# Retention values for all heads first, tokens on partitions, kept in DRAM; sums of output weights beside them

## The chip, the cores and the metric

The kernel runs on one core of a Trainium2 chip. The metric is device microseconds of one execution, the median of several. TensorE (PE in the profile) multiplies; VectorE (DVE) and ScalarE (ACT) add, split and move; GpSimd (POOL) does a few small powers; SyncE (SP) issues the DMAs, all on one queue and in program order. DRAM is reached only by DMA; PE writes PSUM banks of 128 x 512 float32, which DVE or ACT empty.

## The reference

A sequence of 1024 tokens with 1024 features goes through a retention layer and then an attention layer, in float32. The change is in the first:

```
h = rmsnorm(x, g_pre)
q, k, v, gate = split(h @ w_in)         # 1024, 1024, 2048, 2048 columns; 8 heads
q, k = rope(q), rope(k) * 128**-0.5     # a head: q, k of 128 columns, v of 256
for every chunk of 64 tokens, in order:
    inner = (q k^T * inner_dec) v
    cross = (q R) * xi;  R = R * g_c + (k * zeta)^T v
o = groupnorm(inner + cross) * gn_gain  # per head
y = (silu(gate) * o) @ w_out
h = x + rmsnorm(y, g_post)
```

The second layer (latent attention with shared keys and values) reads h and is left as it is.

## The kernel before

**Arithmetic.** A float32 product is made as three matmuls of a high and a low part of each operand (`mm3`, L180). So every operand is split first: ACT rounds it to the high part, DVE subtracts to get the low one (`split`, L187, rows of L189 and L190). On top lies one level of a Strassen-like scheme: a 2 x 2 block product needs seven products instead of eight, with sums of blocks on both sides. On the left these are sums of x's blocks (S1 to S4), on the right sums of weight blocks (T1 to T4), and the results are combined in the bank or by additions on DVE.

**Column pairs.** Layer A's input projection runs over 24 column pairs, three a head: q with k, the two halves of v, the two halves of the gate. Results have features on partitions and tokens along the row. `pair` (L343) runs a pair's seven products, its steps a to g; a `product` (L331) is 12 matmuls of 128 x 512. `Units` (L53) fetches a pair's weights (wraw, two loads of 512 KB), makes T1 to T4 (wsum) and splits each of the seven operands into a unit. Pair 0 is run plainly, with four units and eight products (`plain`, L405), and pairs 1 and 2 (EARLY) in an order that can start before the second half of the tokens is in.

**Heads.** A pair's results go to a sink. The steps of a head's retention are queued from there: `later(n, f)` runs f after n more products, and every product calls `tick`. Per half of the tokens: `ret_scores` transposes k and makes the scores; `ret_values` (L589) brings the values, made with features on partitions (`sink_v`, L524), to tokens on partitions by eight PE transposes (L599) and splits them; `ret_states` updates R; `ret_mix` multiplies, normalises, and its tail transposes y (L694), gates it and stores it to DRAM (yd). So a head's retention runs between the products of the next pairs, and a head is worked off in the time of 21 products.

**Output.** `prepare_out_a` (L720), called before the last pair, queues loads of yl (from yd) and wl (output weights) and makes the sums of the weights on DVE in that pair (L749 to L751; the last, L795, in the output itself). `out_a` runs seven products of four blocks, each of 24 matmuls.

**Order and buffers.** The order on an engine is fixed when the program is built: a scheduler arranges the instructions of the engines within the dependences that the code gives. Large tiles come from one heap of 51 blocks of 128 x 1024 float32, given out again in the order in which they were freed.

Of the kernel before, what the change touches and what calls it, by code (L numbers as in the profile page):

```python
# [18 lines left out]
P = 128  # L19
# [33 lines left out]
class Units:  # L53
# [6 lines left out]
    def __init__(self, T, order, source, ahead, early=0, plain=()):  # L60
# [3 lines left out]
        self.hold = sum(p < early for p, _ in order) - 2  # L64
        self.plain = plain
        self.pairs = list(dict.fromkeys(p for p, _ in order))
        self.raw, self.sums, self.made, self.left, self.ready = {}, {}, {}, {}, deque()

    def fetch(self):
# [12 lines left out]
        self.left[p] = {"r0": 2, "r1": 2} if p in self.plain else {"r0": 3, "r1": 5, "ta": 3, "tb": 3}  # L82
# [28 lines left out]
    def prep(self):  # L111
# [8 lines left out]
        name = {"B11": "r0", "B12": "r0", "B21": "r1", "B22": "r1", "T1": "ta", "T3": "ta", "T2": "tb", "T4": "tb"}[what]  # L120
# [10 lines left out]
    def next(self):  # L131
        if not self.ready:
            self.prep()
        u = self.ready.popleft()
        self.fill()

        if self.at < len(self.order):
            n = self.pairs.index(self.order[self.at][0]) + 2
            if self.at < self.hold:
                n = min(n, self.early)  # L140
            while self.n_fetched < min(n, len(self.pairs)):
                self.fetch()
        return u

# [4 lines left out]
class Trunk:  # L149
# [121 lines left out]
    def run(self):  # L271
# [4 lines left out]
        self.h1 = dp.tile([NT, P, DM], F32, name="h1")  # L276
        self.yd = [[dp.tile([P, DM], F32, name=f"yd{h}_{half}") for half in range(2)] for h in range(NH)]
# [53 lines left out]
    def product(self, ps, units, name, more=False, over=False, unit=None):  # L331
        u = units.next() if unit is None else unit
# [4 lines left out]
        if unit is None:  # L337
            self.heap.free(u)
# [38 lines left out]
    def layer_a(self):  # L377
# [4 lines left out]
        EARLY = 3  # L382
        order = [(0, w) for w in ("B11", "B12", "B21", "B22")]
        order += [(p, w) for p in range(1, EARLY) for w in ("B11", "B21")]
        order += [(p, "T2") for p in range(1, EARLY)]
        order += [(p, w) for p in range(1, EARLY) for w in ("T3", "T4")]
        order += [(p, w) for p in range(1, EARLY) for w in ("T1", "B22")]
        order += [(p, w) for p in range(EARLY, 3 * NH) for w in WINOGRAD]
        units = Units(self, order, lambda p: (I["w_in_a"][p], None), 3, EARLY, (0,))
        self.X, A = {}, {}  # L390
        rows = [[heap.get("xt") for _ in range(HT)] for _ in range(2)]
        for half in range(2):
            for t in range(HT):
                nc.sync.dma_start(rows[half][t], I["x"][half * HALF + t * P:half * HALF + (t + 1) * P, :])
            units.fetch()
        self.rows_norm(rows[0])
        self.rows_in(0, rows[0], A)
        sinks = [(h, kind) for h in range(NH) for kind in "qvg"]
        make = lambda p: getattr(self, "sink_" + sinks[p][1])(sinks[p][0])
        self.heads = [{"h": h} for h in range(NH)]  # L400

        first = make(0)
        us = [units.next() for _ in range(4)]

        def plain(i):  # L405
            banks = [self.bank("acc") for _ in range(2)]
            for m in range(2):
                for j in range(2):
                    self.product(banks[j], units, f"A{i + 1}{m + 1}", more=m > 0, unit=us[2 * m + j])
                    if m:  # L410
                        first(i, j, banks[j], None)

        plain(0)
        self.rows_norm(rows[1])
        pairs = [(make(p), {}) for p in range(1, EARLY)]
        for sink, st in pairs:
            self.pair(units, sink, "ae", st)
            if sink is pairs[0][0]:
                self.rows_in(1, rows[1], A)
                ret = self.small([P, 16], "ret")  # L420
                nc.sync.dma_start(ret, I["ret"])
                self.zeta, self.geps = ret[:, 0:8], ret[:, 8:16]
                self.cs = [heap.get("cos"), heap.get("sin")]
                for i in range(2):
                    nc.sync.dma_start(self.cs[i], I["ropea"][i])
        self.left_sum(A, "S2")
        plain(1)
        heap.free(*us, *[b for hl in self.X.pop("A21") for b in hl])
        for steps, w in (("b", "S3"), ("cf", "S4"), ("dg", None)):
            if w:  # L430
                self.left_sum(A, w)
            for sink, st in pairs:
                self.pair(units, sink, steps, st)
        for p in range(EARLY, 3 * NH):
            if p == 3 * NH - 1:
                self.prepare_out_a()
            self.pair(units, make(p), over=p == 3 * NH - 1)
# [12 lines left out]
    def rows_in(self, half, rows, A):  # L450
# [3 lines left out]
        for n in names:  # L454
            A["S1" if n == "A22" else n] = [heap.get("xa") for _ in range(2)]
            self.X[n] = [(heap.get("xhi", F32R), heap.get("xlo", F32R)) for _ in range(2)]
# [5 lines left out]
        for k in range(KD):  # L462
            if half:
# [7 lines left out]
            hi, lo = self.X[n][m]  # L471
            self.split_scaled(hi[:, c], lo[:, c], pt, g)
# [14 lines left out]
    def sink_q(self, h):  # L487
# [4 lines left out]
        def sink(i, j, bank, U):  # L492
# [4 lines left out]
            if cb[i][1] == 2:  # L497
                st["qk", i] = cb[i][0]
                if h:
                    self.rotate_a(cb[i][0], i)  # L500
                else:
                    self.later(7, lambda: self.rotate_a(cb[i][0], i))
                if i == 0:
                    dm = st["dmask"] = self.small([P, P], "dm", bufs=2)
                    self.nc.sync.dma_start(dm, self.I["dmask"][:, h * P:(h + 1) * P])
                    if h:
                        self.later(4, lambda: self.ret_scores(st, 0))
                        self.later(15 if h < NH - 1 else 11, lambda: self.ret_scores(st, 1))
# [14 lines left out]

    def sink_v(self, h):  # L524
        st = self.heads[h]
        vt = {}

        def sink(i, j, bank, U):
            if i not in vt:
                vt[i] = [self.heap.get("vt"), 0]  # L530
            self.take(vt[i][0][:, j * HALF:(j + 1) * HALF], bank, U)
            vt[i][1] += 1
            if vt[i][1] == 2:
                st["vt", i] = vt[i][0]
                if i == 0:
                    if h == 0:
                        self.later(1, lambda: self.ret_scores(st, 0))
                        self.later(8, lambda: self.ret_scores(st, 1))
                    wait = (2, 4, 6, 10, 12, 14) if h < NH - 1 else (1, 2, 5, 3, 6, 8)
                    for n, (what, half) in zip(wait, [(w, i) for i in range(2) for w in  # L540
                                                      (self.ret_values, self.ret_states, self.ret_mix)]):
                        self.later(n, lambda what=what, half=half: what(st, half))

        return sink
# [43 lines left out]

    def ret_values(self, st, half):  # L589

        nc, heap = self.nc, self.heap
        vt = st["vt", half]
        hi, lo = st["v", half] = heap.get("vhi", F32R), heap.get("vlo", F32R)
        for m in range(2):
            pt = self.bank("r", (P, 2, 256))
            for i in range(2):
                for e in range(2):
                    c = e * HALF + (2 * m + i) * P
                    nc.tensor.transpose(pt[:, i, e * P:(e + 1) * P], vt[:, c:c + P], self.ident)  # L599
            c = slice(m * HALF, (m + 1) * HALF)  # L600
            self.split(hi[:, c], lo[:, c], pt.rearrange("p a b -> p (a b)"))
# [118 lines left out]
    def prepare_out_a(self):  # L720
# [19 lines left out]
        K = [{"uses": 2} for _ in range(4)]  # L740

        def weights(b):
            k = K[b]
            k["b11"], k["b12"], k["b22"] = right(0, 0, b), right(0, 1, b), right(1, 1, b)

        def sums(b):
            k = K[b]
            k["t1"] = heap.get("t1")
            sub(k["t1"], k["b12"], k["b11"])  # L749
            sub(k["b12"], k["b22"], k["b12"])  # L750
            sub(k["b22"], k["b22"], k["t1"])  # L751
            k["t3"], k["t2"] = k.pop("b12"), k.pop("b22")
            used(b)

        def used(b):
            K[b]["uses"] -= 1
            if not K[b]["uses"]:
                heap.free(K[b].pop("b11"))

        for b in range(4):  # L760
            self.later(2 + 3 * b, lambda b=b: weights(b))
            self.later(3 + 3 * b, lambda b=b: sums(b))

        def load(prod, b):
            k = K[b]
            if prod == 1:
                k["a11"] = left(0, 0, b)
            elif prod == 6:
                k["a21"], k["a22"], k["a11"] = left(1, 0, b), left(1, 1, b), left(0, 0, b)
            elif prod == 4:  # L770
                k["a22"], k["b21"] = left(1, 1, b), right(1, 0, b)
# [5 lines left out]
        def make(prod, b):  # L777
            k = K[b]
            if prod == 1:
                u = two(k["a11"], k["b11"], k.pop("a11"))  # L780
                used(b)
                return u
# [660 lines left out]
```

## Time and profile before

| | us |
|---|---|
| median of 3 runs (1293.27 to 1294.65) | 1294.58 |
| the profiled execution | 1292.86 |
| its span in the trace | 1291.1 |
| PE busy | 1257.4 |
| DVE busy | 1001.7 |
| ACT busy | 642.8 |

The profile is of one execution; times inside it are counted from its span's start. Layer A's projection and retention run from the start to 598.67 us, where the first output product begins; the output and the second layer follow. A row of a group shows line, engine, operation, output and inputs by the names of the program, count, busy time, mean duration, and idle time before with what ended it. In a timeline row the bracket holds the idle time before it and its releaser. Matmuls overlap: one may show 0.39 us and yet follow the one before by 0.23.

### The profile page before, as it was taken

What the parts mean: (1) busy time and instruction counts of PE and PEld (TensorE: products, weight loads), DVE (VectorE), ACT (ScalarE), POOL (GpSimd) and SP (SyncE); (2) the same over time, 40 slices, a digit from 0 to 9 for tenths busy, and PEclk for the clock granted to TensorE, in tenths of its full rate; (3) what the DMA queues carried; (4) which work ended last, traced back from release to release, by engine and by line L of the source; (5) the groups of instructions that cost most, each with busy time, mean ns of one, the idle gap of its engine ahead of it and who ended that gap; (6) DMA issues with size and microseconds to landing.
All of it is one profiled execution on the core that took longest, in us unless ns stands there. A gap on an engine that the chain in (4) does not pass through costs nothing. (4 is left out here: it accounts for less than half of the span.)

```text
span 1291.1 us, 17796 instructions
## 1 busy us (share of the span) xinstructions
PE 1257.4 (97%) x6708; PEld 1082.5 (84%) x6708; DVE 1001.7 (78%) x1879; ACT 642.8 (50%) x1177; POOL 72.3 (6%) x86
## 2 busy tenths in 40 slices
PE   6999999999999999999999999999999999999997
PEld 5888888888888888888888779978898989898886
DVE  6988887787968787789986885686588888889622
ACT  8645453544545453545543865544355545456411
POOL 1000100000000000001000231200000000000000
PEclk9999999999999999999999999989999999999999
DMA  6021121121112021138237631032502011122321
GB/s 266 5 94 52 49 84 49 52 82 51 67 30 87 34 84 50 50 100 308 97 137 253 228 144 46 1 130 76 202 11 57 13 34 36 33 77 98 109 88 49
DMA packets 36246, 113.38 MB, mean 88 GB/s; under 512 B 4928, under 2 KB 5952, under 8 KB 36160
## 3 DMA queue, kind: packets, MB, share of 16 engines
q1 hardware_dynamic: 36160, 112.25, 24.9%
q8 instruction: 52, 0.85, 0.3%
q14 instruction: 34, 0.28, 0.1%
HBM read 88.11 MB, written 19.92 MB: 84 GB/s over the span
## 5 line engine op out<-in xcount | busy, mean ns | idle before, releaser
L183 PE MATMUL acc<-xhi,unit 128*128 128x512 f32 x788 | 313.5, 398 | 5.7 <-DVE gT L1061 2.8
L184 PE MATMUL acc<-xlo,unit 128*128 128x512 f32 x788 | 309.1, 392 | 0.3 <-DVE xlo L190 0.3
L185 PE MATMUL acc<-xhi,unit 128*128 128x512 f32 x788 | 308.3, 392 | 0.0
L183 PEld LDWEIGHTS acc<-xhi,unit 128*128 128x128 f32 x788 | 148.9, 189 | 35.5 <-ACT xhi L189 3.2
L185 PEld LDWEIGHTS acc<-xhi,unit 128*128 128x128 f32 x788 | 148.6, 189 | 31.5
L184 PEld LDWEIGHTS acc<-xlo,unit 128*128 128x128 f32 x788 | 148.9, 189 | 28.9 <-DVE xlo L190 0.8
L189 ACT ACTIVATE unit<-wsum 128x512 fp32r<-128x512 f32 x108 | 67.4, 629 | 40.4 <-PE acc L185 13.3
L190 DVE TENSOR_TENSOR unit<-wsum,unit 128x512 fp32r<-128x512 f32 x108 | 71.9, 682 | 19.8 <-ACT unit L189 19.7
L189 ACT ACTIVATE unit<-wraw 128x512 fp32r<-128x512 f32 x85 | 53.4, 634 | 55.6 <-DVE yT L697 17.4
L1245 ACT ACTIVATE p<-S,nm 128x896 f32<-128x896 f32 (+3 forms) x64 | 47.3, 740 | 54.4 <-DVE nm L1242 47.6
L190 DVE TENSOR_TENSOR unit<-wraw,unit 128x512 fp32r<-128x512 f32 x85 | 57.7, 684 | 9.3 <-ACT unit L189 9.2
L189 ACT ACTIVATE pT<-r 128x512 fp32r<-128x512 f32 (+2 forms) x96 | 44.5, 488 | 37.6 <-PE r L1275 37.5
L667 POOL TENSOR_TENSOR rg<-rg,mhalf 128x2 f32<-128x2 f32 x32 | 30.6, 955 | 548.9 <-DVE rg L666 546.3
L190 DVE TENSOR_TENSOR pT<-r,pT 128x512 fp32r<-128x512 f32 (+2 forms) x96 | 50.8, 548 | 4.9 <-ACT pT L189 4.6
L183 PE MATMUL acc<-thi,slo 128*128 128x512 f32 x128 | 50.1, 393 | 1.2 <-DVE slo L190 1.2
L183 PE MATMUL acc<-whi,u 128*128 128x512 f32 x128 | 50.0, 391 | 0.0
L184 PE MATMUL acc<-wlo,u 128*128 128x512 f32 x128 | 49.8, 389 | 0.0
L184 PE MATMUL acc<-tlo,shi 128*128 128x512 f32 x128 | 49.8, 390 | 0.0
L185 PE MATMUL acc<-whi,u 128*128 128x512 f32 x128 | 49.8, 390 | 0.0
L185 PE MATMUL acc<-thi,shi 128*128 128x512 f32 x128 | 49.7, 390 | 0.0
L1242 DVE TENSOR_REDUCE nm<-S 128x1 f32<-128x896 f32 (+3 forms) x64 | 47.5, 743 | 1.0
L184 PE MATMUL acc<-pT,v 128*128 128x256 f32 x160 | 46.0, 288 | 0.1
(283 smaller groups left out, 3091.1 us busy)
## 6 DMA issues: line engine op xcount, KB each, us to landing
wraw<-in_w_in_a_dram SPq DMA_DIRECT2D x48, 512.0 KB, 3.8
yl<-yd SPq DMA_DIRECT2D x28, 512.0 KB, 5.0
wl<-in_w_out_a_dram SPq DMA_DIRECT2D x24, 512.0 KB, 4.2
yd<-yT SPq DMA_DIRECT2D x16, 512.0 KB, 3.0
xt<-in_x_dram SPq DMA_DIRECT2D x8, 512.0 KB, 7.4
xres<-in_x_dram SPq DMA_DIRECT2D x8, 512.0 KB, 5.7
h<-xres SPq DMA_DIRECT2D x8, 512.0 KB, 3.6
wraw<-in_w_gate_dram SPq DMA_DIRECT2D x8, 512.0 KB, 3.5
```

The source lines that it names most:

```text
L183: mm(ps, lhs[1], rhs[0], start=first, stop=False, skip_group_check=more)
L184: mm(ps, lhs[0], rhs[1], start=False, stop=False, skip_group_check=more)
L185: mm(ps, lhs[0], rhs[0], start=False, stop=last, skip_group_check=more)
L189: self.nc.scalar.activation(hi, src, AF.Copy)
L190: self.nc.vector.tensor_sub(lo, src, hi.bitcast(F32))
L667: nc.gpsimd.tensor_tensor(out=rg, in0=rg, in1=self.mhalf[:, 0:1].to_broadcast([P, 2]), op=ALU.pow)
L1242: nc.vector.tensor_reduce(out=nm, in_=view, op=ALU.max, axis=AX.XY, negate=True)
L1245: nc.scalar.activation(p[:, :w].rearrange("p (a b) -> p a b", a=pieces), view, AF.Exp, bias=nm, accum_out=sm)
```

## The change

The values of all heads are made before the heads, by a class and a function of their own. The slices of x now stand still in PE and 512 columns of value weights move through, so that the results have tokens on partitions. There are two groups of four heads, each with the seven products of the scheme, each product in four token tiles of 12 matmuls: 672 matmuls, as many as eight value pairs had. The order of the 14 steps is: B11 and B21 of both groups, then T2, T3, T4, T1, B22 of the first, then of the second. Results go to DRAM (vd, 32 stores of 256 KB with rows of 1 KB), and each head loads its own again (vt, 16 loads of 512 KB). There they are only split; the transposes and `sink_v` are gone.

At four of the 14 steps (`OUT`) `out_sums` loads four blocks of output weights, makes the four sums on DVE and stores them in DRAM (td). The output loads those instead of making them.

The heads keep two column pairs, q with k and the gate, all with seven products. Retention steps are queued over 14 products a head instead of 21. `plain` and the early pairs are gone.

```diff
+class WideUnits:
+        self.steps = [(g, w) for g in range(n_groups) for w in ("B11", "B21")]
+        self.steps += [(g, w) for g in range(n_groups) for w in ("T2", "T3", "T4", "T1", "B22")]
...
+    def load(self, i):
+        g, w = self.steps[i]
+        for q in {"B11": ("B11",), "B21": ("B21",), "T2": ("B11", "B12", "B22"), "T4": ("B21",), "B22": ("B22",)}.get(w, ()):
+            self.raw[g][q] = [T.heap.get("wv") for _ in range(2)]
+            for b, r in enumerate(self.raw[g][q]):
+                T.nc.sync.dma_start(r, self.what(g, int(q[1]) - 1, int(q[2]) - 1, b))
+
+    def prep(self):
+        if w == "T2":
+            for b in range(2):
+                b11, b12, b22 = (R[q][b] for q in ("B11", "B12", "B22"))
+                sub(b11, b12, b11)
+                sub(b12, b22, b12)
+                sub(b22, b22, b11)
+        if w == "T4":
+            for b in range(2):
+                sub(R["B21"][b], R["B21"][b], R["T2"][b])
...
+        for r in R[w]:
+            hi, lo = T.heap.get("vhi", F32R), T.heap.get("vlo", F32R)
+            T.split(hi, lo, r)
...
+    def values_a(self, wide, rows, A, units):
+        def put(g, i, j, t, bank, U):
+            if t % 2 == 0:
+                part[i, j] = heap.get("vo")
+            o = part[i, j]
+            self.take(o[:, (t % 2) * HALF:(t % 2 + 1) * HALF], bank, U)
+            if t % 2:
+                v = o.rearrange("p (t h e) -> p t h e", t=2, h=2)
+                for k in range(2):
+                    dst = self.vd[4 * g + 2 * j + k][i].rearrange("p (t e) -> p t e", t=HT)
+                    nc.sync.dma_start(dst[:, t - 1:t + 1, :], v[:, :, k, :])
...
+        OUT = (6, 10, 11, 12)
+        for s, (g, w) in enumerate(wide.steps):
+            wide.load(s + 2)
+            us = ready.popleft()
+            for t in range(HT):
+                for b in range(2):
+                    for e in range(2):
+                        self.mm3(ps, [y[:, c] for y in x[b]], [u[:, e * HALF:(e + 1) * HALF] for u in us[b]],
+                                 not more and k == 0, k == 3, more)
+                if s in OUT and t in (0, 2):
+                    self.out_sums(OUT.index(s), t)
+                if t == 0:
+                    if s + 1 < len(wide.steps):
+                        ready.append(wide.prep())
+                    else:
+                        units.fetch()
+                if s + 1 == len(wide.steps) and t == 2:
+                    units.fill()
...
+    def out_sums(self, b, part):
+        if not part:
+            self.wo4 = [heap.get("wl") for _ in range(4)]
+            for w, (j, n) in zip(self.wo4, ((0, 0), (0, 1), (1, 1), (1, 0))):
+                nc.sync.dma_start(w, self.I["w_out_a"][j, n, b])
+            return
+        b11, b12, b22, b21 = self.wo4
+        sub(b11, b12, b11)
+        sub(b12, b22, b12)
+        sub(b22, b22, b11)
+        sub(b21, b21, b22)
+        for n, w in enumerate((b11, b22, b12, b21)):
+            nc.sync.dma_start(self.td[n][b], w)
...
+        order = [(p, w) for p in range(2 * NH) for w in WINOGRAD]
+        sinks = [(h, kind) for h in range(NH) for kind in "qg"]
...
+                    wait = (1, 2, 4, 6, 8, 9, 11, 13) if h < NH - 1 else (1, 2, 3, 5, 4, 6, 8, 10)
+                    steps = (self.ret_scores, self.ret_values, self.ret_states, self.ret_mix)
...
+    def ret_load(self, st, half):
+        v = st["vt", half] = self.heap.get("vt")
+        self.nc.sync.dma_start(v, self.vd[st["h"]][half])
...
     def ret_values(self, st, half):
         hi, lo = st["v", half] = heap.get("vhi", F32R), heap.get("vlo", F32R)
-        for m in range(2):
-            pt = self.bank("r", (P, 2, 256))
-            for i in range(2):
-                for e in range(2):
-                    c = e * HALF + (2 * m + i) * P
-                    nc.tensor.transpose(pt[:, i, e * P:(e + 1) * P], vt[:, c:c + P], self.ident)
-            c = slice(m * HALF, (m + 1) * HALF)
-            self.split(hi[:, c], lo[:, c], pt.rearrange("p a b -> p (a b)"))
+        self.split(hi, lo, vt)
...
+        def summed(n, b):
+            t = heap.get("wl")
+            nc.sync.dma_start(t, self.td[n - 1][b])
+            return t
...
             elif prod == 6:
                 k["a21"], k["a22"], k["a11"] = left(1, 0, b), left(1, 1, b), left(0, 0, b)
+                k["t2"] = summed(2, b)
+            elif prod == 7:
+                k["t3"] = summed(3, b)
```

On PE, in a head of before, these rows stand between two products (unit is a split weight operand, vt the values with features on partitions):

```order
L185 MATMUL acc_2322<-xhi_583,unit_2227 128x512
L599 MATMUL r_2340<-ident_88,vt_1967 128x128 x4
L599 MATMUL r_2347<-ident_88,vt_1967 128x128 x4
L183 MATMUL acc_2356<-xhi_587,unit_2253 128x512
L184 MATMUL acc_2356<-xlo_588,unit_2253 128x512
```

In the changed kernel the transposes of k and y remain in a head (L675, L792), and the state update (`z`) reads split values that PE had no part in; here on PE in the first head, from a product's end through the state update:

```order
L233 MATMUL acc_1988<-xhi_684,unit_1897 128x512
L231 MATMUL r_2011<-vhi_1951,z_235_1915 128x256
L232 MATMUL r_2011<-vlo_1952,z_235_1915 128x256
L233 MATMUL r_2011<-vhi_1951,z_235_1915 128x256
L231 MATMUL r_2011<-vhi_1951,z_235_1915 128x256
```

What fell out are two groups of eight transposes a head; vhi and vlo now come from a wide split of the reloaded vt.

On SP, near the end of the values stage of the changed kernel (wl: output weights, td: their sums, vd: values, wraw: the first head's weights):

```order
L547 DMA wl_1346<-in_w_out_a_dram 128x1024
L474 DMA vd_1_93<-vo_1359 128x2x256
L474 DMA vd_1_95<-vo_1359 128x2x256
L555 DMA td_3_67<-wl_1343 128x1024
L555 DMA td_3_75<-wl_1344 128x1024
L555 DMA td_3_71<-wl_1345 128x1024
L555 DMA td_3_79<-wl_1346 128x1024
L474 DMA vd_1_93<-vo_1400 128x2x256
L474 DMA vd_1_95<-vo_1400 128x2x256
L75 DMA wraw_1433<-in_w_in_a_dram 128x1024
```

Before, on SP in the heads, a pair's loads stood between the loads and stores of other pairs and heads:

```order
L78 DMA wraw_3027<-in_w_in_a_dram 128x1024
L78 DMA wraw_3028<-in_w_in_a_dram 128x1024
L700 DMA yd_0_70<-yT_2974 128x1024
L78 DMA wraw_3265<-in_w_in_a_dram 128x1024
L78 DMA wraw_3264<-in_w_in_a_dram 128x1024
```

The heads' first load now stands behind the last stores of the sums, each of which follows a DVE operation.

On DVE, in the last step with output sums of the changed kernel (L522 and L527 empty PE's banks into u, L608 into vo; L550 to L553 are the sums):

```order
L550 TENSOR_TENSOR wl_1343<-wl_1344,wl_1343 128x1024
L608 TENSOR_TENSOR vo_1400<-acc_1379,u_1157 128x512
L551 TENSOR_TENSOR wl_1344<-wl_1345,wl_1344 128x1024
L527 TENSOR_TENSOR u_443<-acc_1379,u_443 128x512
L552 TENSOR_TENSOR wl_1345<-wl_1345,wl_1343 128x1024
L608 TENSOR_TENSOR vo_1400<-acc_1403,u_1157 128x512
L553 TENSOR_TENSOR wl_1346<-wl_1346,wl_1345 128x1024
L527 TENSOR_TENSOR u_443<-acc_1403,u_443 128x512
```

Before, the same sums stood in the last pair (L749 to L751), between unit splits and the steps of the last heads:

```order
L750 TENSOR_TENSOR wl_5434<-wl_5436,wl_5434 128x1024
L356 TENSOR_TENSOR u_476_5387<-acc_5389,u_476_5387 128x512
L637 COPY R_5405<-r_5406 128x256
L751 TENSOR_TENSOR wl_5436<-wl_5436,t_538_5471 128x1024
L190 TENSOR_TENSOR r_530_5421<-R_5405,r_530_5421 128x256
```

So the sums moved from the last head's pair to the value steps, and the additions that free banks stand alternately with them.

More of the change, by code (lines that the diff above doesn't have):

```diff
@@ L53, with __init__ @@
 class Units:
-    def __init__(self, T, order, source, ahead, early=0, plain=()):
+    def __init__(self, T, order, source, ahead, early=0):
         self.T, self.order, self.source, self.ahead, self.early = T, order, source, ahead, early
         self.at = self.n_fetched = 0
-        self.hold = sum(p < early for p, _ in order) - 2
-        self.plain = plain
         self.pairs = list(dict.fromkeys(p for p, _ in order))
@@ L81, in fetch @@
                 T.nc.vector.tensor_mul(v, v, gains[:, None, 4 * j:4 * j + 4, None].to_broadcast([P, 2, 4, P]))
[L82 removed]
+        self.left[p] = {"r0": 3, "r1": 5, "ta": 3, "tb": 3}
     def done(self, p, *names):
@@ L276, in run @@
         self.h1 = dp.tile([NT, P, DM], F32, name="h1")
+        self.td = [[dp.tile([P, DM], F32, name=f"td{n}_{b}") for b in range(4)] for n in range(4)]
+        self.vd = [[dp.tile([P, DM], F32, name=f"vd{h}_{half}") for half in range(2)] for h in range(NH)]
         self.yd = [[dp.tile([P, DM], F32, name=f"yd{h}_{half}") for half in range(2)] for h in range(NH)]
@@ L329, in left_sum, with product @@
             self.heap.free(*A["S1"])
-    def product(self, ps, units, name, more=False, over=False, unit=None):
-        u = units.next() if unit is None else unit
+    def product(self, ps, units, name, more=False, over=False):
+        u = units.next()
         for k in range(4):
@@ L336, in product @@
                      not more and k == 0, k == 3, more)
-        if unit is None:
-            self.heap.free(u)
+        self.heap.free(u)
         if over:
@@ L381, in layer_a @@
         make_identity(nc, self.ident)
[L382 to L389, printed above, removed]
         self.X, A = {}, {}
+        wide = WideUnits(self, NH // 4, lambda g, j, n, b: I["w_v"][g, j, n, b])
         rows = [[heap.get("xt") for _ in range(HT)] for _ in range(2)]
@@ L394, in layer_a @@
                 nc.sync.dma_start(rows[half][t], I["x"][half * HALF + t * P:half * HALF + (t + 1) * P, :])
-            units.fetch()
+            wide.load(half)
         self.rows_norm(rows[0])
-        self.rows_in(0, rows[0], A)
-        sinks = [(h, kind) for h in range(NH) for kind in "qvg"]
-        make = lambda p: getattr(self, "sink_" + sinks[p][1])(sinks[p][0])
-        self.heads = [{"h": h} for h in range(NH)]
-        first = make(0)
-        us = [units.next() for _ in range(4)]
@@ L405, in plain @@
-        def plain(i):
-            banks = [self.bank("acc") for _ in range(2)]
-            for m in range(2):
[L408 to L423, printed above, removed]
-                for i in range(2):
-                    nc.sync.dma_start(self.cs[i], I["ropea"][i])
@@ L426, in layer_a @@
[L426 to L435, printed above, removed]
-                self.prepare_out_a()
-            self.pair(units, make(p), over=p == 3 * NH - 1)
+        self.rows_in(0, rows[0], A, lambda: self.rows_norm(rows[1]))
@@ new lines, in layer_a @@
+        order = [(p, w) for p in range(2 * NH) for w in WINOGRAD]
+        units = Units(self, order, lambda p: (I["w_in_a"][p], None), 3)
+        self.values_a(wide, rows[1], A, units)
+        sinks = [(h, kind) for h in range(NH) for kind in "qg"]
+        self.heads = [{"h": h} for h in range(NH)]
+        for p, (h, kind) in enumerate(sinks):
+            if p == 2 * NH - 1:
+                self.prepare_out_a()
+            self.pair(units, getattr(self, "sink_" + kind)(h), over=p == 2 * NH - 1)
@@ L448, in rows_norm, with rows_in @@
             nc.vector.tensor_scalar_mul(x, x, r)
-    def rows_in(self, half, rows, A):
+    def rows_in(self, half, rows, A, between=None):
         nc, heap = self.nc, self.heap
@@ L455, in rows_in @@
             A["S1" if n == "A22" else n] = [heap.get("xa") for _ in range(2)]
-            self.X[n] = [(heap.get("xhi", F32R), heap.get("xlo", F32R)) for _ in range(2)]
+            if n != "A21":
+                self.X[n] = [(heap.get("xhi", F32R), heap.get("xlo", F32R)) for _ in range(2)]
         banks = [self.bank("r" if half or k >= 4 else "acc") for k in range(KD)] if not half else []
@@ L462, in rows_in @@
         for k in range(KD):
+            if between and k == KD // 2:
+                between()
             if half:
@@ L505, in sink @@
                     self.nc.sync.dma_start(dm, self.I["dmask"][:, h * P:(h + 1) * P])
-                    if h:
-                        self.later(4, lambda: self.ret_scores(st, 0))
-                        self.later(15 if h < NH - 1 else 11, lambda: self.ret_scores(st, 1))
+                    wait = (1, 2, 4, 6, 8, 9, 11, 13) if h < NH - 1 else (1, 2, 3, 5, 4, 6, 8, 10)
+                    steps = (self.ret_scores, self.ret_values, self.ret_states, self.ret_mix)
+                    for n, (what, half) in zip(wait, [(w, i) for i in range(2) for w in steps]):
+                        self.later(n, lambda what=what, half=half: what(st, half))
+                    self.ret_load(st, 0)
+                    self.later(wait[5] - 3, lambda: self.ret_load(st, 1))
         return sink
@@ L522, in rotate_a @@
         heap.free(xs)
[L524 to L544, printed above, removed]
     def sink_g(self, h):
@@ L738, in two @@
             return u
[L740 to L762, printed above, removed]
+        K = [{} for _ in range(4)]
+        def summed(n, b):
+            t = heap.get("wl")
+            nc.sync.dma_start(t, self.td[n - 1][b])
+            return t
         def load(prod, b):
```

112 lines of the change are left out of this document (91 added, 21 removed).

## The prediction

> **What bounds the kernel now.** I read the page first: its busy shares, then its slices.
>
> ```profile
> span 1291.1 us, 17796 instructions
> PE 1257.4 (97%) x6708; PEld 1082.5 (84%) x6708; DVE 1001.7 (78%) x1879; ACT 642.8 (50%) x1177; POOL 72.3 (6%) x86
> ...
> PE   6999999999999999999999999999999999999997
> ...
> DVE  6988887787968787789986885686588888889622
> ...
> PEclk9999999999999999999999999989999999999999
> DMA  6021121121112021138237631032502011122321
> GB/s 266 5 94 52 49 84 49 52 82 51 67 30 87 34 84 50 50 100 308 97 137 253 228 144 46 1 130 76 202 11 57 13 34 36 33 77 98 109 88 49
> ```
>
> TensorE is busy in nine tenths or more of every slice but the ends, at full granted clock. So the time is the number of matmuls by their spacing, plus a few gaps. The second engine is DVE, and it comes closest to full just where layer A ends. The windows answer says how close (length, busy PE, PEld, DVE, ACT, POOL, clock, DMA share, GB/s):
>
> ```profile
> 0.00:10.00 10.00, 1.62 (x8) 1.62 (x9) 2.07 (x8) 6.07 (x10) 2.61 (x9) 1.00 0.80 292
> 16.00:166.00 150.00, 148.31 (x755) 124.72 (x756) 131.84 (x226) 90.70 (x152) 9.22 (x10) 1.00 0.18 64
> 367.00:439.50 72.50, 71.71 (x376) 61.04 (x375) 57.08 (x109) 34.72 (x60) 3.85 (x4) 1.00 0.17 60
> 439.50:512.00 72.50, 71.72 (x376) 61.07 (x375) 57.08 (x109) 34.73 (x60) 3.51 (x4) 1.00 0.17 60
> 580.00:599.00 19.00, 19.00 (x109) 16.51 (x108) 17.68 (x38) 13.46 (x21) 1.38 (x2) 1.00 0.81 276
> 599.00:667.00 68.00, 67.98 (x320) 56.58 (x319) 64.95 (x74) 33.60 (x41) 2.27 (x2) 1.00 0.40 148
> 667.00:715.00 48.00, 48.00 (x213) 39.77 (x212) 35.96 (x39) 18.14 (x21) 1.11 (x2) 1.00 0.65 228
> ```
>
> The third and fourth rows are one head each; I cut them at the copy that sets R, which DVE makes once a head:
>
> ```profile
> 367.00 0.42 DVE L637 COPY R<-r 128x256 f32<-128x256 f32 x1
> ...
> 439.52 0.42 DVE L637 COPY R<-r 128x256 f32<-128x256 f32 x1
> ```
>
> So a head takes 72.5 us; PE idles 0.8 of it, DVE works 57.1. What one matmul costs is its spacing, not its duration, since they overlap. The timeline shows the first and the last of 60 products in a row, then a group of eight value transposes with their neighbour, and the head's one gap:
>
> ```profile
> 16.31 0.50 PE L183 MATMUL acc<-xhi,unit 128*128 128x512 f32 x1 [2.69 <-ACT xa L478]
> ...
> 29.86 0.39 PE L185 MATMUL acc<-xhi,unit 128*128 128x512 f32 x1
> ...
> 315.71 1.04 PE L599 MATMUL r<-ident,vt 128*128 128x128 f32 x8
> 316.50 0.48 PE L183 MATMUL acc<-xhi,unit 128*128 128x512 f32 x1
> ...
> 413.53 0.44 PE L694 MATMUL r<-ident,y 128*128 128x128 f32 x2 [0.79 <-ACT y L677]
> ```
>
> A product matmul takes (29.86 - 16.31)/59 = 0.230 us, a product of 12 takes 2.76, a pair of seven 19.3. Eight transposes hold PE for 0.79, so one takes 0.099.
>
> **What goes from PE.** All 128 value transposes go (the row of the tile vt, below): 128 x 0.099 = **12.7 us**. Pair 0 ran eight products and now seven: 12 x 0.230 = **2.8**. Otherwise the matmuls are as many: 672 of values stand for 8 value pairs of 84. PE had hardly a gap, so this is time on the path: **-15.5 us** if nothing comes in its place.
>
> ```profile
> L599 PE MATMUL r<-ident,vt x128: 270/272/273, 66.8 to 582.6; 128*128 128x128 f32 x128
> ```
>
> [...] Summed as cost it would make 35 us here, but the spacing just read is 99 ns, and I keep 12.7.
>
> **The head loop.** A head becomes 72.5 - 1.59 (16 transposes) - 19.3 (its value pair) = **51.6 us**, with its gap of 0.8 still in it. For DVE I take spacings again:
>
> ```profile
> 320.13 0.68 DVE L105 TENSOR_TENSOR wsum<-wraw,wraw 128x512 f32<-128x512 f32 x1
> 320.73 0.68 DVE L106 TENSOR_TENSOR wsum<-wraw,wsum 128x512 f32<-128x512 f32 x1
> ...
> 329.62 1.22 DVE L519 TENSOR_TENSOR qk<-qk,cos 128x1024 f32<-128x1024 f32 x1
> 330.77 1.22 DVE L520 TENSOR_TENSOR xs<-xs,sin 128x1024 f32<-128x1024 f32 x1
> ```
>
> That is 0.60 for 128x512, 1.15 for 128x1024. With the value pair go seven unit splits, four weight sums and five additions, 16 x 0.60 = 9.6; the four vlo splits become two wide ones, 2.4 against 2.3. DVE is left with 57.1 - 9.7 = **47.4 of 51.6**, 92% where it was 79%. ACT's share stays near half. Bounds on the gaps: none left (-6.3 over eight heads), or DVE bound (the first rival, +25). The row nearest in load is 599 to 667, where DVE works 96% and PE loses 0.02; 16 to 166, with 88% and waits of the same kinds, loses 1.7 of 150. I take **+1** over all heads, the last, compressed head included.
>
> **Start.** PE's first product waited 2.69 for ACT. In the changed order one ACT operation more stands ahead of it, and the weights come as splits of 1024 columns. One narrow ACT split has a row of 0.63, so **+0.6**, between nothing and 2.7 (the same wait twice).
>
> ```profile
> L189 ACT ACTIVATE unit<-wsum 128x512 fp32r<-128x512 f32 x108 | 67.4, 629 | 40.4 <-PE acc L185 13.3
> ```
>
> **Values stage.** 672 matmuls are 154 us of PE. DVE gets 48 additions (28.8), 28 wide splits, 16 sums of value weights and 16 of output weights (60 x 1.15 = 69), and about 32 of x's rows by the order: some 129, 84%, less than the 88% of the window from 16 to 166 above. That row lost 1.7 in 150, at the same kind of work; bounds are -1.7 and +7.6 (a transfer rival, below). The change adds two waits here. SP's stores wait for the DVE operation that fills their block, and behind them on SP stand the next loads; DVE's output sums wait for loads of `wl`, and behind them on DVE stand the additions that empty PE's banks and the splits that PE takes next. So a load that lands late would pass through DVE to PE. A step lasts 11 us, the sums stand two tiles (5.5 us) behind their loads, and a `wl` load took 4.2 us (row below): covered, with about 1 us to spare where the queue is short. I take **+2**, the nearest being the early window's 1.7, for wide splits that stand late behind additions and for one late group of loads.
>
> **From values to heads.** In the last four steps (4 x 48 x 0.230 = 44 us) SP issues 12 loads and 12 stores of 512 KB for the output sums, 3.1 MB of values, and 3 to 4 MB of weights and tables: some 19 MB. The best stretch of the trace is the load at the start, the slices at 404 to 431 here:
>
> ```profile
> GB/s 0 92 328 412 415 412 431 404 418 410 410 407 407 391 399 362 4 0 0 11 0 5 5 0 0 0 0 0 0 0 0 0 0 0 11 0 0 0 0 0
> ```
>
> At 410 GB/s, 19 MB take 46 us. The first head's weights (wraw) stand on SP behind the last four stores of sums, which wait for DVE; before, such a load was issued a whole pair ahead. So cover is nearly gone: one step of 11 us has to hold the queue's rest, the landing and a DVE split.
>
> The page's rows of issue to landing, and from the answer on 600 to 700 us the slices of GB/s and one smaller load:
>
> ```profile
> wraw<-in_w_in_a_dram SPq DMA_DIRECT2D x48, 512.0 KB, 3.8
> yl<-yd SPq DMA_DIRECT2D x28, 512.0 KB, 5.0
> wl<-in_w_out_a_dram SPq DMA_DIRECT2D x24, 512.0 KB, 4.2
> yd<-yT SPq DMA_DIRECT2D x16, 512.0 KB, 3.0
> ...
> GB/s 382 390 415 374 167 315 210 336 362 113 0 0 0 0 0 0 0 0 0 7 0 3 0 67 352 70 349 29 370 229 246 356 373 377 208 320 118 303 220 287
> ...
> wraw<-in_w_kv_a_dram SPq DMA_DIRECT2D x1, 480.0 KB, 7.7
> ```
>
> Bounds: nothing, or 17 (second rival). I take **+2.8**: the 2 us by which 46 passes 44, and 0.8 for an ACT and DVE split whose first half overlaps the landing. PE waits for it with nothing else to do, since the last value products are done by then and all that is left of the stage, their additions and stores, is no matmul. Inside the loop the sixteen reloads of values are each a 512 KB load, issued three products (8.3 us) ahead of their split, against 5.0 for `yl`; they are hidden.
>
> **The end of layer A.** The sums' 16 DVE operations leave the last pair (16 x 1.15 = 18 us of DVE time), which gains PE nothing: between 580 and 599 us, where part of them ran, it was busy without a gap. In their place product 6 of the output loads four blocks a step, 2.1 MB in 24 x 0.230 = 5.5 us, 381 GB/s; the trace's 600 to 625 us, the first loads of `yl`, move 167 to 415 in their first nine slices, and the window from 599 on shows PE idle for 0.02 us of it. At the 292 GB/s of the first ten us the four steps would take 7.2 each instead of 5.5, 7 in all: between nothing and +7. I take **+1.5**, near the lower end, since the first blocks can be loaded ahead of the last pair's end.
>
> **Sum.** -12.7 - 2.8 + 0.6 + 2 + 2.8 + 1 + 1.5 = -7.6. The profiled execution took 1292.86 (1.8 beyond its span), so it would take 1285.3. The median of the runs shown is 1294.58, 1.7 above; I forecast **1287.0** for the median.
>
> **Rivals.**
>
> *DVE bounds the heads (slower).* These are DVE's waits in one head before, on ACT and POOL, which less PE work does not shorten:
>
> ```profile
> DVE unit L190 <- ACT unit L189: 2.7, 4, 1.0
> ...
> DVE r L190 <- ACT r L189: 1.7, 2, 1.2
> DVE nb L674 <- POOL rg L667: 1.7, 3, 0.6
> DVE z L195 <- ACT z L194: 1.2, 1, 1.2
> ```
>
> They sum to 7.3. If they all stay, DVE's period is 47.4 + 7.3 = 54.7; above 51.6 DVE decides, 3.1 a head, 25 in all: 1287.0 - 1 + 25 = **1311**. Against it: such waits mostly arise because DVE runs ahead, and vanish when work is queued. For it: R's chain (copy, ACT split, DVE split) is serial. [...]
>
> *Transfers bound the last value steps (slower or level).* The value stores have rows of 1 KB, unlike any of before. How much they lose no row shows. Landings spread by two (7.7 us for the 480 KB of kv weights, 3.8 for 512 KB of w_in), so I bound them by half rate: 3.1 MB cost 7.6 more, and at 355 GB/s, as in the slices of `yl`, 19 MB take 53.5: 61 against 44 us, **+17** instead of +2.8, giving **1301**; half of that is **1294**, level. It decides once SP's queue is late by more than the one step of cover. For it: shares of 0.99 are never held outside the start. Against: only the head's first weights are needed at once.
>
> *All of it counts (faster still).* The gaps of 0.8 go with the new spacing of steps, and start, transition and end are covered: -15.5 - 6.3 = **1273** at most, some 1278 as a case.
>
> That the transposes were free anyway is excluded: PE idles 0.8 of 72.5.
>
> **How the numbers follow.** Forecast (1283 to 1291.9) 0.48; all of it 0.15; level, by part of the transfers, 0.17; transfers in full 0.12; DVE bound 0.08. Within 0.2% of before, about what a measurement of this kernel tells from no change, means 1292.0 to 1297.2. So faster 0.63, same 0.17, slower 0.20. The range 1277 to 1302 leaves out DVE bound and the tail of "all of it".
>
> **What would show it.** In the changed profile: no L599-like transposes of vt; the R copy every 51 to 52 us (54 or more is the first rival); PE's idle between the last value matmul and the first unit product about 3 us, released by `wraw` or its split (over 10 is the second); PE idle in the value steps about 2 us more than before; output product 6 with gaps of DMA release near 1.5. A wait of PE on ACT or POOL once a half head that I have not listed, times sixteen, would make the forecast wrong most easily.

## The result, and the profile after

The changed kernel takes **1272.68 us** (median of 4 runs, 1271.9 to 1274.58) against 1294.62 (4 runs) beside it: ratio 0.9833, 95% interval 0.9816 to 0.985. That is 21.9 us less, where 7.6 less was forecast, and outside the stated range. Its profiled execution took 1271.9.

The page of the changed kernel, with the lines that answer to those of before:

```profile
span 1270.1 us, 17662 instructions
PE 1239.4 (98%) x6568; PEld 1067.2 (84%) x6568; DVE 1002.8 (79%) x1835; ACT 628.7 (49%) x1130; POOL 64.6 (5%) x86
...
DVE  5978878898998998999966874685688798989622
...
DMA  9248981232222312248662630214301010123321
```

PE is busy 18.0 us less and idle 3.0 us less. DVE's total is unchanged; in the heads it now stands at nine tenths. The DMA engines are loaded in the fourth to sixth slice (95 to 190 us: 0.90 busy, 318 GB/s), the second half of the value steps.

Two marks show where the 21.0 us of the span went: the first transposes of hn, with which the second layer starts, in the timeline of before and of the changed kernel:

```profile
723.91 0.33 PE L918 MATMUL acc<-ident,hn 128*128 128x128 f32 x1 [0.33 <-ACT hn L910]
```

```profile
704.01 2.23 PE L1001 MATMUL acc<-ident,hn 128*128 128x128 f32 x16 [0.39 <-ACT hn L993]
```

Of the 21.0 us, 19.9 came in the retention layer and 1.1 in the second, which the change leaves alone (last section). All of PE's larger gaps after its first matmul and before that mark, in the changed kernel:

```profile
16.41 0.50 PE L231 MATMUL acc<-vhi,xlo 128*128 128x512 f32 x1 [2.33 <-ACT xa L601]
30.70 0.50 PE L231 MATMUL acc<-vhi,xlo 128*128 128x512 f32 x1 [1.32 <-ACT u L516]
175.56 0.50 PE L231 MATMUL acc<-xhi,unit 128*128 128x512 f32 x1 [1.34 <-DVE unit L238]
204.56 0.41 PE L675 MATMUL r<-ident,qk 128*128 128x128 f32 x2 [0.40 <-DVE qk L644]
```

They are the start, the second value step (which waits for copies of the first one's banks), the passage to the heads and the first scores, 5.4 us in all; before there were 8.8 (2.69, 1.19, 0.18, and six of about 0.79 at the transposes of y, L694). The heads, the last pair and the output have none. The windows answer shows the value steps' end, one head (cut at R's copy, 313.47 to 364.38), and the output's first stretch (length, PE, PEld, DVE, ACT, POOL, clock, DMA share, GB/s):

```profile
131.00:175.50 44.50, 43.22 (x191) 35.48 (x189) 33.57 (x39) 6.41 (x8) 0.00 (x0) 1.00 0.92 327
...
313.47:364.38 50.91, 50.86 (x276) 43.64 (x275) 46.06 (x91) 28.33 (x49) 3.05 (x4) 1.00 0.25 84
...
578.00:646.00 68.00, 68.00 (x325) 57.03 (x324) 61.48 (x78) 35.32 (x44) 2.88 (x3) 1.00 0.75 272
```

A head takes 50.9 us, forecast 51.6; DVE works 46.1 of them and PE idles 0.05.

### The profile page after: what moved, and what is told of

Same layout as the page of the kernel before. It is cut to its first block, busy times and chain, and to the rows that moved or that the text cites. A ratio compares the mean times of both kernels' runs of the same rounds, so it can differ in the third digit from the quotient of the medians.

```text
span 1270.1 us, 17662 instructions
## 1 busy us (share of the span) xinstructions
PE 1239.4 (98%) x6568; PEld 1067.2 (84%) x6568; DVE 1002.8 (79%) x1835; ACT 628.7 (49%) x1130; POOL 64.6 (5%) x86
## 5 line engine op out<-in xcount | busy, mean ns | idle before, releaser
L231 PE MATMUL acc<-xhi,unit 128*128 128x512 f32 x560 | 221.0, 395 | 4.2 <-DVE gT L1144 2.8
L232 PE MATMUL acc<-xlo,unit 128*128 128x512 f32 x560 | 220.0, 393 | 0.6 <-DVE xlo L238 0.6
L233 PE MATMUL acc<-xhi,unit 128*128 128x512 f32 x560 | 218.9, 391 | 0.0
L231 PEld LDWEIGHTS acc<-xhi,unit 128*128 128x128 f32 x560 | 105.7, 189 | 26.0 <-ACT xhi L237 3.2
L233 PEld LDWEIGHTS acc<-xhi,unit 128*128 128x128 f32 x560 | 105.6, 189 | 22.0
L232 PEld LDWEIGHTS acc<-xlo,unit 128*128 128x128 f32 x560 | 105.7, 189 | 20.2 <-DVE xlo L238 0.9
L231 PE MATMUL acc<-vhi,xlo 128*128 128x512 f32 x224 | 87.2, 391 | 3.7 <-ACT xa L601 2.3
L233 PE MATMUL acc<-vhi,xhi 128*128 128x512 f32 x224 | 87.2, 389 | 0.0
L232 PE MATMUL acc<-vlo,xhi 128*128 128x512 f32 x224 | 87.2, 389 | 0.0
L1328 ACT ACTIVATE p<-S,nm 128x896 f32<-128x896 f32 (+3 forms) x64 | 47.4, 741 | 55.5 <-DVE nm L1325 49.1
L237 ACT ACTIVATE unit<-wraw 128x512 fp32r<-128x512 f32 x60 | 37.7, 631 | 56.0 <-issue 21.9
L237 ACT ACTIVATE pT<-r 128x512 fp32r<-128x512 f32 (+2 forms) x96 | 44.5, 489 | 37.2 <-PE r L1358 37.0
L237 ACT ACTIVATE vhi<-wv 128x1024 fp32r<-128x1024 f32 x28 | 29.2, 1062 | 65.0 <-PE acc L232 16.3
L238 DVE TENSOR_TENSOR pT<-r,pT 128x512 fp32r<-128x512 f32 (+2 forms) x96 | 50.9, 549 | 4.8 <-ACT pT L237 4.5
L231 PEld LDWEIGHTS acc<-vhi,xlo 128*128 128x128 f32 x224 | 42.1, 188 | 12.7 <-ACT xa L601 2.6
L231 PE MATMUL acc<-whi,u 128*128 128x512 f32 x128 | 50.0, 391 | 0.0
```

The lines of the kernel that those rows point to most:

```text
L231: mm(ps, lhs[1], rhs[0], start=first, stop=False, skip_group_check=more)
L232: mm(ps, lhs[0], rhs[1], start=False, stop=False, skip_group_check=more)
L233: mm(ps, lhs[0], rhs[0], start=False, stop=last, skip_group_check=more)
L237: self.nc.scalar.activation(hi, src, AF.Copy)
L238: self.nc.vector.tensor_sub(lo, src, hi.bitcast(F32))
L1328: nc.scalar.activation(p[:, :w].rearrange("p (a b) -> p a b", a=pieces), view, AF.Exp, bias=nm, accum_out=sm)
```

## The experiments

Layer A's end below is always the mark above: in two executions of the changed kernel it stands at 704.01 and 704.65, where the whole time varies by one or two us.

**The transposes alone.** From the kernel before:

```diff
-                    nc.tensor.transpose(pt[:, i, e * P:(e + 1) * P], vt[:, c:c + P], self.ident)
...
-            self.split(hi[:, c], lo[:, c], pt.rearrange("p a b -> p (a b)"))
+            self.split(hi[:, c], lo[:, c], vt[:, c])
```

> The kernel before without the PE transposes of the values: what stands with features on partitions is split as it is, so the retention multiplies by values in the wrong layout. Theory A (a group of eight transposes costs PE 0.885 us, its neighbour's slower start included: 315.47 to 316.81 us in the trace of before, less two matmul spacings of 0.2275): 16 groups x 0.885 = 14.2 us less, layer A's end (the first transposes of hn, 723.91 us before) at about 709.7, the six gaps of 0.79 at the transposes of y still there. Theory B, as recorded (0.099 a transpose): 12.7 us less, end at 711.2. Theory C (the transposes also made the gaps, by holding PSUM banks that the mix needs): gaps gone too, 14.2 + 4.7 = 19 us less, end at 705.

Measured: ratio to before 0.989 (0.9871 to 0.9909). One head, and the mark:

```profile
359.17:429.92 70.75, 69.94 (x360) 59.37 (x359) 56.68 (x109) 34.78 (x60) 3.85 (x4) 1.00 0.17 61
```

```profile
710.02 0.33 PE L913 MATMUL acc<-ident,hn 128*128 128x128 f32 x1 [0.55 <-ACT hn L905]
```

The head is 1.76 us shorter for 16 transposes, 0.11 each, and the mark 13.9 earlier: theory A. The gap stays (69.94 busy of 70.75), so theory C falls. The predicted 0.099 left out that behind such a group the first matmul holds off the second for 0.31 us (316.50 to 316.81 before), 0.08 more than the usual 0.23.

**The gap at the transposes of y.** From the kernel before:

```diff
-        self.later(3, tail)
+        self.later(4, tail)
```

> The kernel before with the tail of a half (transposes of y, gate, store) queued four products after the mix instead of three. Theory A (the gap of 0.79 a head is the chain mix, statistics, power on POOL, normalising on ACT, 10.0 us from the mix's end at 403.94 to the last y at 413.93, against three products of PE work, 8.2 us; a fourth product covers it): the six gaps go, 4.7 us less, layer A ends at about 719.2. Theory B (DVE and ACT are late in any case and the wait comes back at another operand): no gain, layer A's end within 1 us of 723.91.

Measured: ratio to before 0.9941 (0.9922 to 0.996), the mark at 717.53, 6.4 earlier. One head, then the last y on ACT and the transposes on PE in the next:

```profile
363.94:435.39 71.45, 71.45 (x376) 61.18 (x375) 56.84 (x109) 34.23 (x60) 3.86 (x4) 1.00 0.18 61
```

```profile
409.96 1.02 ACT L677 ACTIVATE y<-r,nb,rg 128x256 f32<-128x256 f32 x2
```

```profile
411.81 1.04 PE L694 MATMUL r<-ident,y 128*128 128x128 f32 x8
```

All six gaps went: theory A. The chain from the second mix of a head to its last y still takes 9.9 us (the mix ends at 401.1, y at 411.0), but PE now comes 10.7 behind the mix. The head is shorter by 1.05, not 0.79: at the gap, the y transposes were issued in pieces between matmuls (two, a product matmul, two more, from 413.53 to 414.18), and by the difference that cost another 0.26. In the changed kernel PE comes 8.7 and 14.1 us behind the two mixes of a head, and finds y ready. Here are the second mix's last matmul, its last two y and its transposes:

```profile
344.37 0.28 PE L233 MATMUL r<-r,q 128*128 128x256 f32 x1
...
350.93 1.02 ACT L775 ACTIVATE y<-r,nb,rg 128x256 f32<-128x256 f32 x2
...
358.58 0.60 PE L792 MATMUL r<-ident,y 128*128 128x128 f32 x4
```

The chain itself is shorter there too, 7.5 us from the mix's end to the last y (6.3 behind the first mix; before, 10.0 and 4.5). So its shorter queue of steps did by the way what one number does here, and by these numbers the shorter chain alone would have been enough; why it is shorter stays open.

**The sums back in the last pair.** In the changed kernel, `prepare_out_a` of before is put back and this is taken out:

```diff
-                if s in OUT and t in (0, 2):
-                    self.out_sums(OUT.index(s), t)
```

> The changed kernel with the sums of output weights made in the last pair and the output again, as before, and none beside the values; values still go through DRAM. Theory A (moved sums matter because the last head is worked off in 14 products: DVE is busy 56.9 of 61.0 us from 517.05 to 578 and 61.5 of 68 after it, and 16 more operations of 1.15, 18 us, go into some 10 us of room): PE waits at the end of the heads and in the first output products, layer A's end 5 to 10 us later than 704.01; the gap of 1.34 between values and heads goes or shrinks, since twelve stores leave the queue. Theory B (the sums were hidden in the last pair and are hidden now): layer A's end 1 to 2 us earlier than 704.01, by that gap alone.

Measured: 1281.33 us, ratio to before 0.9912 (0.989 to 0.9933). PE's waits that the changed kernel doesn't have, and the stretch of the first outputs:

```profile
PE r L231 <- DVE slo L238: 3.2, 1, 3.2
...
PE acc L231 <- DVE slo L238: 2.3, 2, 1.7
...
PE acc L232 <- DVE tlo L238: 1.7, 1, 1.7
...
PE r L231 <- DVE R L735: 0.9, 1, 0.9
```

```profile
576.00:644.00 68.00, 61.50 (x278) 50.59 (x277) 64.98 (x85) 32.34 (x41) 6.67 (x4) 0.95 0.38 138
```

Theory A: 7.4 us of new gaps (one of the 2.3, 0.6, is in every run), all released by DVE in the last head and the first outputs, against 1.34 gone before the heads and 1.32 gone at 30.70. The mark is 9.9 us later; the rest is the clock, at half in three intervals of 3.41 us (last section). Two make the 0.95 of that stretch, 3.4 us of work; the third, 1.7, stands at the first products. So the moved sums are a part of the gain that only counts together with the shorter heads: before, with 21 products in a head, they stood in the last pair and PE did not wait (19.00 us busy of the 19.00 from 580 on).

**Room on DVE.** In the changed kernel, per half of a head, three and six times:

```diff
+        for _ in range(3):
+            self.nc.vector.tensor_max(self.cs[0][:, :HALF], self.cs[0][:, :HALF], self.cs[0][:, :HALF])
```

> The changed kernel with six more DVE operations of 128x512 a head (the maximum of a table with itself, so nothing else changes), 6 x 0.60 = 3.6 us. Theory A (DVE has room until its busy time fills the period): 46.1 + 3.6 = 49.7 of 50.88 us, head period longer by no more than 0.3. Theory B (the first rival of the prediction: DVE's waits, 4.3 us a head here, stay and add to its busy time): 46.1 + 3.6 + 4.3 = 54.0, head period longer by 3.1.

> The changed kernel with twelve such DVE operations a head, 7.2 us. Theory A: 46.1 + 7.2 = 53.3, over the period of 50.88, so DVE decides and the head takes 53.3 to 54, 2.4 to 3.1 us longer, some 18 to 24 us in all. Theory B: 57.6, 6.7 us longer a head, some 50 in all.

Measured, with one execution each, 1289.61 and 1300.88 us; the head by the windows answer is 52.37 with three and 54.29 with six:

```profile
369.57:421.94 52.37, 50.93 (x275) 43.70 (x275) 48.77 (x98) 27.89 (x49) 3.86 (x4) 1.00 0.26 82
```

```profile
375.81:430.10 54.29, 52.38 (x275) 43.51 (x275) 52.20 (x104) 27.91 (x48) 3.87 (x4) 1.00 0.26 79
```

The first is a miss for both theories: 1.5 longer, though DVE idles 3.6. All of it is one wait of PE, at the first state update of a head. It is shown with the DVE operations that PE waits for (`cos` is the table, so the first is an added one); the same place in the changed kernel is below, DVE's split first:

```profile
366.04 0.68 DVE L700 TENSOR_TENSOR cos<-cos 128x512 f32<-128x512 f32 x1
366.63 1.22 DVE L238 TENSOR_TENSOR vlo<-vt,vhi 128x1024 fp32r<-128x1024 f32 x1
```

```profile
368.00 0.35 PE L232 MATMUL r<-vlo,z 128*128 128x256 f32 x1 [1.44 <-DVE vlo L238]
```

```profile
362.05 1.21 DVE L238 TENSOR_TENSOR vlo<-vt,vhi 128x1024 fp32r<-128x1024 f32 x1
```

```profile
363.57 0.28 PE L232 MATMUL r<-vlo,z 128*128 128x256 f32 x1
```

There the split ends 0.3 us before PE uses it. Three added operations, 1.8 us, stand ahead of it in a run of DVE work without a gap, and 1.8 less 0.3 is the 1.5. So 0.3 us of room at that place decides, not the 4.8 us that DVE idles over the head. The second, 3.4 longer, lies a little beyond theory A's upper end of 3.1, with DVE at 96%: the same wait of 1.44 stands in it, and the rest is in waits of 0.2 and less and in late starts. The marks come 14.3 and 29.3 us later, more than the heads make; waits in the first outputs and intervals at half clock are in it. Theory B, the first rival with waits added to busy time, is wrong in both: DVE's waits shrink as it fills, from 4.3 us a head in the changed kernel to 3.6 and 2.1.

**Room for transfers.** In the changed kernel:

```diff
         for n, w in enumerate((b11, b22, b12, b21)):
+            nc.sync.dma_start(self.td2[n][b], w)
             nc.sync.dma_start(self.td[n][b], w)
```

> The changed kernel with every sum of output weights stored twice, the second time to a place that nobody reads: 8.4 MB more to write, 6.3 of them in the last four value steps, where the changed kernel moves 327 GB/s x 44.5 us = 14.6 MB. Theory A (only the place on SP of the first head's weights counts): they stand behind four more stores of 512 KB, 2.1 MB at 400 GB/s, 5.2 us: the gap before the first head grows from 1.34 to about 6.5, and the value steps have no gap. Theory B (the transfers bound the steps themselves): 20.9 MB at 400 GB/s take 52 us against 44, and gaps of 8 us or more stand inside the value steps as well.

Measured, in one execution: 1293.92 us. The gap before the first head, the stretch ahead of it and the gap's own:

```profile
194.15 0.80 PE L231 MATMUL acc<-xhi,unit 128*128 128x512 f32 x1 [14.09 <-DVE unit L238]
```

```profile
150.00:180.00 30.00, 28.21 (x123) 22.53 (x121) 21.13 (x24) 4.07 (x4) 0.00 (x0) 1.00 0.95 354
180.00:194.00 14.00, 0.06 (x1) 0.00 (x0) 2.58 (x4) 1.19 (x2) 0.00 (x0) 0.59 1.00 350
```

The gap grew by 12.75, where theory A said 5; inside the value steps there are only 3.5 us of small ones, where theory B said 8 or more. Together 16.2 for 8.4 MB. Of this, 14.5 fall to the last four steps (12.75 and 1.8 of the small ones), where 6.3 MB at the 354 GB/s of that window are 17.8. The DMA engines are busy 0.95 and then all of the time. So bandwidth it is, as in B, but the delay is passed down SP's queue and falls due at its end, as in A. By the difference the changed kernel has some 3 us to spare in these steps. The mark comes at 725.66, 21.7 later; most of what the gaps leave is the clock, at half from 182.6, inside the large gap, to 199.7, 5.6 us behind it.

**The first head's weights earlier.** In the changed kernel (the second kernel also made the first two copies of the first value step on DVE):

```diff
+            if s == len(wide.steps) - 2:
+                units.fetch()
             wide.load(s + 2)
...
-                    else:
-                        units.fetch()
-                if s + 1 == len(wide.steps) and t == 2:
+                if s + 1 == len(wide.steps) and t == 1:
```

> The changed kernel with only the first head's weights fetched one value step earlier, ahead of the last loads of output weights, and split one tile earlier; all else as in the changed kernel. Theory A (place on SP): the gap of 1.34 before the first head goes and nothing comes in its place; the copy of R in the first head at about 207.9 instead of 209.28, and 1.3 us less than the changed kernel run beside it.

> The changed kernel with the first head's weights fetched one value step earlier, ahead of the last loads of output weights, and split one tile earlier, and with the first two copies of the first value step's banks made on DVE instead of ACT. Theory A (the gap of 1.34 before the first head is that load's place on SP behind the last four stores of sums, and the gap of 1.32 at 30.70 us is ACT's copy standing behind two wide splits): both go, 2.6 us less, layer A's end at about 701.4, ratio to the changed kernel about 0.998. Theory B (the gaps are DMA bandwidth and ACT's load; they come back at the next load or split): end within 0.7 us of 704.01.

> The changed kernel once more, to stand beside the one with the early fetch on the same chip: ratio to before 0.983 as measured, within 0.001.

Measured: 1270.18 us (5 runs, 1269.68 to 1271.89) with the early fetch, 1272.32 (1271.29 to 1272.47) for the changed kernel beside it; ratios to before 0.9825 and 0.9835. SP's rows of the changed kernel show the place; behind them R's first copy, in the changed kernel and with the early fetch:

```profile
161.28 5.52 SPq L555 DMA_DIRECT2D td<-wl  x4
166.85 1.70 SPq L474 DMA_DIRECT2D vd<-vo  x2
168.65 0.44 SPq L75 DMA_DIRECT2D wraw<-in_w_in_a_dram  x1
...
209.28 0.41 DVE L735 COPY R<-r 128x256 f32<-128x256 f32 x1
```

```profile
207.08 0.42 DVE L735 COPY R<-r 128x256 f32<-128x256 f32 x1
```

The four stores hold SP for 5.5 us, waiting for DVE's sums; the load goes out at 168.65 and lands five us later. Issued at 154.09 it leaves no gap. R's first copy comes 2.2 us earlier, where 1.4 was expected, and the mark, at 702.45, 1.6. This is the fastest of the kernels by median, 0.17% below the changed one, though the two ranges overlap. The second kernel took 1270.49 (ratio 0.9827). Its gap before the heads went too, and its mark, 703.20, is 1.45 before the 704.65 of the changed kernel's second execution, which that gap (1.39 there) covers. What its copies on DVE are worth it does not show: it waits 0.51 at 29.94 for DVE's split of value weights, but in its execution and in that of the changed kernel the clock is at half for 3.41 us at the first products, and the changed kernel then has no gap at 31 us either.

## Why the prediction was wrong

The sign and the removed work were right; the costs set against it were not. Term by term, in us of layer A:

| term | forecast | measured | by |
|---|---|---|---|
| 128 transposes | -12.7 | -14 | e1, 8 x 1.76 |
| one product of pair 0 | -2.8 | -2.7 | 12 spacings of 0.227; not run alone |
| start | +0.6 | 0 | first product at 16.41 against 16.31 |
| value steps | +2 | 0 | one gap of 1.32 for two of 1.37 before |
| values to heads | +2.8 | +1.3 | e9 and the gap of 1.34 |
| heads | +1 | -4 | worked out: six gaps gone, 6 x 1.05 as in e2; 0.4 at the first scores and some 2 (0.2 a head) given back |
| end | +1.5 | 0 | no gap from 204.97 to 704 |

These sum to -19.4 of 19.9.

**The step that failed** is "A head becomes 72.5 - 1.59 (16 transposes) - 19.3 (its value pair) = **51.6 us**, with its gap of 0.8 still in it", followed by "I take **+1** over all heads". The gap was carried over as a property of the head. It was a race between a chain of 10.0 us and three products of PE work, 8.2 us, and the change moves both runners: to 7.5 and 14.1 us. In the order of the changed kernel the second y transposes stand behind the scores of the next head, four and a half products behind their mix. In layer A the forecast missed by 12.3 us; this step makes 5 of them, the four costs below 5.6, the transposes 1.3. By the parts measured, a head would be 72.5 - 1.76 - 1.05 - 19.0 = 50.7; it is 50.9, and what the last 0.2 a head is made of stays open.

**The other four costs** were each taken inside their bounds but above what came. All four lay on transfers or splits that might be late; only one was. For the passage to the heads the mechanism was right (the load behind the stores on SP) and the size was not: 19 MB were counted into four steps, where the window from 131.00 shows 44.5 us at 327 GB/s, 14.6 MB. Part of the loads had gone out before. With the load issued earlier (e9) nothing waits, so the 2 us by which the transfers were to pass the products did not arise.

**The rivals.** The case that "all of it counts" gave 1273 at most and was given a chance of 0.15; it is what came. That the two numbers lie 0.3 us apart is luck, though: the case counts eight gaps of 0.8, where six stood and each was worth 1.05; the transposes gave 1.3 more than in its sum, and 1.3 stayed before the heads; and 1.1 us came outside layer A. DVE bounding the heads was wrong as worked out (by its own terms DVE is left with 57.1 - 9.6 + 0.1 = 47.6 us a head, not 47.4; it measured 46.1), but e4 shows how near another form of it was. Transfers bounding the last value steps did not come either, and e7 shows how near they were: 8.4 MB more cost 16.2 us in gaps and 21.7 by the mark, as much as the whole gain.

## What to carry to other kernels

A gap that an engine shows at a fixed place can be a race; before carrying it over, time the chain (here mix to y, 10.0 us) and the work between (three products, 8.2), and look in the new order for both. An engine's idle share says little about its room: 0.3 us ahead of one split counted, not 4.8 us of idle time. And on a queue that issues in order, a load that starts the next stage belongs ahead of stores that wait for arithmetic (here four of them held SP for 5.5 us; with the load ahead of them a gap of 1.34 went).

## What the runs showed of the hardware

The granted clock drops in the second layer, which is the same in all kernels, around a gap of PE that all of them have there, and not by the same amount: to 0.95 before and 0.98 after, over 70 us (the page of before has it as the one 8 in its row PEclk). Before and after, that gap and the stretch around it:

```profile
854.52 0.77 PE L183 MATMUL acc<-xhi,unit 128*128 128x512 f32 x1 [2.82 <-DVE gT L1061]
```

```profile
834.10 0.47 PE L231 MATMUL acc<-xhi,unit 128*128 128x512 f32 x1 [2.82 <-DVE gT L1144]
```

```profile
800.00:870.00 70.00, 66.91 (x356) 60.22 (x356) 48.68 (x81) 33.81 (x65) 8.24 (x9) 0.95 0.17 61
```

```profile
800.00:870.00 70.00, 66.61 (x313) 56.60 (x313) 53.55 (x76) 32.05 (x57) 5.12 (x4) 0.98 0.22 76
```

The clock records of these traces have one interval at half speed there, of 6.8 us before and 3.4 after, which is 1.7 us of work apart, enough for the 1.1 us gained in a layer that was not changed. It is not shown to be all of it: from the mark to the end, the traces with the short interval take 565.6 to 566.8 us, those with the long one 566.5 to 569.5. All such intervals in the traces, but the one at a trace's end, are multiples of 3.41 us. In the 3.4 us of the changed kernel (from 835.16) the matmuls of a product follow each other by 0.43 us instead of 0.23. What starts an interval no run shows, and the gaps beside them can be short: in the kernel with the sums put back, the clock falls to 0.95 around two gaps of 1.7 us and one of 3.2, and with twelve DVE operations more a head one such interval begins in a gap of 1.44. Nor does every such gap bring one: the other heads of that kernel have the same gap at full clock (1.00 from 321.59 to 375.81, with its 1.44 at 371.82, and from there to 430.10), and four of the eleven traces have an interval at the first products, behind a gap of 2.1 to 2.3, where the others have none. So 1.7 us (half of 3.41) came now and then beside a gap, on top of what it shows, and a difference of 1.7 us between two single executions of these kernels proves nothing.
